# Padding SBUF arrays to one place modulo 512 bytes, and splitting MLP activations of a K tile pair together, in a two-layer decoder trunk

## The chip, the cores and the metric

One core of one Trainium2 chip runs the whole kernel. The metric is the device time in microseconds of that core, as the median of timed runs. The profile is one more execution, taken by the hardware profiler.

## What is computed

The input x is 256 tokens by 2048 features in float32. Two layers run, each with a mixer and a squared-ReLU MLP, and every sub-layer ends in x <- LN(alpha x + f(x)).

```python
bcu = x @ w_in                       # 2048 -> 6144: gate_b, gate_c, u
y = causal_conv3(gate_c * u)         # depthwise, width 3
mix = (gate_b * y) @ w_out           # layer 0
mix = mla(x, shared latent k and v)  # layer 1: 16 heads, rank 512 latents, w_o 2048 -> 2048
mlp(x) = square(relu(x @ w1)) @ w2   # 2048 -> 8192 -> 2048, both layers
```

The weights are read once: some 381 MB of float32 in 512 KB blocks.

## The kernel before

**Two-part numbers.** Every float32 operand of a large product is split into a high part, cast to float32r, and a low part, the rest (`split`, L109, and `put_split`, L306): one cast on ACT and one subtraction on DVE. A product then takes hi x hi, lo x hi and hi x lo and drops lo x lo.

**Weights.** `stream` (L64 to L83) lists all weight blocks in the order of use. `take` (L171) hands out the next ones and prepares blocks some way ahead (LOOK, 5): `load_raw` issues the DMA on SP's queue into one of five raw buffers, and `split` fills one of eight hi and eight lo buffers of 128 x 1024.

**Up products.** `products` (L230) computes one 128-feature tile after another with the weight block stationary. The activations lie as 512 columns, the high half beside the low one, so `high` (L190) streams 512 columns through the high weights and `low` (L194) 256 columns through the low weights: a pair of matmuls for each of the 16 K tiles. Their PSUM tile is ps_u.

**MLP.** `mlp` (L523) runs eight stages q of 1024 hidden features. In a stage, eight up tiles (K from xhl) are evacuated by `hidden` (L558): `whole` adds the two halves of PSUM, ACT does ReLU and square, and `put_split` writes the tile h[m] of array h (tag c, high columns beside low ones). Then the down products run with the activations stationary and 512 columns of w2 moving: `dot` (L245) is three matmuls, L247 hi x hi, L248 x high by w low, L249 x low by w high. Blocks n of 512 outputs accumulate in acc through `put`.

**Fast stages.** In 13 of the 16 stages (`FAST`) the first two output blocks use seven products instead of eight of 2 x 2 blocks (Strassen's scheme in Winograd's form): `down_fast` (L287, PSUM ps_f, 84 matmuls a stage); the other two use `down` (PSUM ps_d, 96). The sums S1 to S4 of a K tile pair are made in `hidden` from the two fh tiles into sf and split into the array `forms` (tag a2). The sums of the weights, T1 to T4, are made in `prepare` (L150 to L165) from two raw loads per pair: L154 makes T1 and T3 in a third raw buffer (raw_t) as soon as the second load is there, L157 and L160 follow, and T4 is split last into its own tile t4 in the pool `fast`. The first product of a pair (factor "4") uses T4.

**The last stage.** `to_out` (L866) loads gbt, the last norm's gain and bias spread to 128 partitions: four DMAs of 512 KB from POOL's queue (L869), into the array with tag b, which xhl used until the last up matmul.

**Where the order comes from.** All instructions are recorded through a tile framework that orders each engine's queue by its own costs; waits follow from the tiles. Each engine then works its queue in that order. `Norm.prepare` (L358) puts one float32 product, mu0p (L365), on PE before a sub-layer's sums begin.

**Places in SBUF.** Pools lie one behind the other, and each tile takes its size rounded up to 32 bytes per partition. So odd sizes (vec 736 bytes, col 16, the arrays xd 16512 or 33024) shift all that follows. The place of an array's first byte modulo 512 in the two programs is:

| array (tag) | before | after |
|---|---|---|
| raw, hi, lo: weights | 384 | 128 |
| conv input xhl0, K tiles 0 to 7 (a1) and acc | 384 | 128 |
| conv input xhl0, K tiles 8 to 15, and forms (a2) | 0 | 128 |
| z, xhl of both MLPs, oT (b) | 128 | 128 |
| h, latents (c) | 384 | 128 |
| sf | 256 | 128 |
| t4 | 256 | 128 |
| xres, S, Q, fh, evac | 384 | 128 |
| ones, identity, cos, sin, mask | 352 | 128 |

A 128-column block is 512 bytes long, so every block of an array has its array's place; only xd, with rows of 2064 bytes, runs through many.

Of the kernel before, what the change touches and what calls it, by code (L numbers as in the profile page):

```python
# [9 lines left out]
F32 = mybir.dt.float32  # L10
F32R = mybir.dt.float32r
AF = mybir.ActivationFunctionType
ALU = mybir.AluOpType
# [26 lines left out]
WO_G = 3  # L40

C_G, C_B, C_CW, C_QG, C_KG, C_END = 0, 64, 128, 176, 180, 184


@with_exitstack
def trunk(ctx: ExitStack, tc: tile.TileContext, xT, vecs, w_in, w_out, w_kv, w_q, w_uk, w_uv,
# [9 lines left out]
    pmm = ctx.enter_context(tc.tile_pool(name="pmm", bufs=4, space=PS))  # L56


    def halves(w):
# [128 lines left out]
    def high(ps, w, blk, x, first):  # L188

        nc.tensor.matmul(ps, w[blk // 8][0][:, blk % 8, :], x, start=first, stop=False)  # L190
# [4 lines left out]

    def mm_run(wps, x, k0, k1, nk, tiles_first=False):
# [32 lines left out]

    def products(n, x, group=0, cuts=()):  # L230

        ws = group_of(group)
        at = [0, *cuts, NC]
        for k0, k1 in zip(at, at[1:]):
            if ws:
                mm_run(ws, x, k0, k1, NC, tiles_first=True)
        yield from [ps for _, ps in ws]
        for i in range(group, n):
            w = take()
            ps = psum("ps_u")  # L240
            mm_run([(w, ps)], x, 0, NC, NC)
            yield ps
# [8 lines left out]
    def held(x, t):  # L251

        return [x[:, o + t * P:o + (t + 1) * P] for o in (0, T)]

# [56 lines left out]

    vec = const.tile([P, C_END], F32, name="vec")
    cos_t = const.tile([P, T], F32, name="cos_t")
# [33 lines left out]
    class Norm:  # L347
# [35 lines left out]
        def widen(self, *tags):  # L383

            n = NC // len(tags)
            self.xd = []
            v = vec[:, C_G:C_G + 128].rearrange("p (v i m) -> p m i v", v=2, i=4)[:, :, self.idx, :]
            for i, tag in enumerate(tags):
                x = act.tile([P, n, 2 * W], F32R, tag=tag, name=f"xd{self.idx}_{i}")
# [74 lines left out]
    def summed(ln, pss, add, m0=0):  # L464

        for m, ps in enumerate(pss, m0):
# [7 lines left out]
    xres = act.tile([P, NC, T], F32, tag="xres", name="xres")  # L474
    xhl = [t[:, k, :] for t in [act.tile([P, NC // 2, 2 * T], F32R, tag=a, name=f"xhl0_{a}") for a in ("a1", "a2")]
           for k in range(NC // 2)]

    first = act.tile([P, 2 * GROUP, 1024], F32, tag="b", name="first")
    for half, cuts in enumerate(FIRST):
# [12 lines left out]

    zt = act.tile([P, NC, 2 * T], F32R, tag="b", name="z")
    z = [zt[:, k, :] for k in range(NC)]
    cbuf = act.tile([P, 2, 5, T + 2], F32, tag="c", name="cbuf")
    pss = products(3 * NC, xhl, GROUP, (2, 4, 8, 12))
# [26 lines left out]
    def mlp(idx, ln, begin, blocks, fast):  # L523

        xt = act.tile([P, NC, 2 * T], F32R, tag="b", name=f"xhl{idx}")
        xhl = [xt[:, k, :] for k in range(NC)]
# [19 lines left out]
        for q in range(NQ):  # L548
            ht = act.tile([P, QC, 2 * T], F32R, tag="c", name=f"h{idx}_{q}")
            h = [ht[:, k, :] for k in range(QC)]  # L550
            forms = None
            if q in FAST[idx // 2]:
                forms = act.tile([P, QC // 2, 2, 4 * P], F32R, tag="a2", name=f"forms{idx}_{q}")
            if q == NQ - 1:
                begin(block)
            pair = []

            def hidden(m, ps, evac, *func):  # L558
                f = tmp.tile([P, T], F32, tag="fh", name="fh", bufs=3)
                evac(ps, f, *func)  # L560
                if not func:
                    nc.scalar.activation(f, f, AF.Relu)  # L562
                nc.scalar.activation(f, f, AF.Square)
                put_split(h[m], f)
                pair.append(f)
                if forms is not None and m % 2:
                    (a11, a21), (a12, a22) = ((v[:, :P], v[:, P:]) for v in pair[-2:])
                    sf = fast.tile([P, 4, P], F32, tag="sf", name="sf")
                    s1, s2, s3, s4 = (sf[:, i, :] for i in range(4))
                    nc.vector.tensor_tensor(s1, a21, a22, ALU.add)  # L570
                    nc.vector.tensor_tensor(s3, a21, a11, ALU.subtract)
                    nc.vector.tensor_tensor(s2, s1, a11, ALU.subtract)
                    nc.vector.tensor_tensor(s4, a12, s2, ALU.subtract)
                    split(forms[:, m // 2, 0, :], forms[:, m // 2, 1, :], sf.rearrange("p i c -> p (i c)"))

            if q == 0:
                for m in range(QC):
# [12 lines left out]
                    if m > 0:  # L590
                        normal()
                acc = act.tile([P, 2, D], F32, tag="a1", name=f"acc{idx}")
            else:
# [57 lines left out]
    with tc.tile_pool(name="att", bufs=1) as ap:  # L651
        lat = act.tile([P, 2 * NK, 2 * T], F32R, tag="c", name="lat")
        chl, qhl = ([lat[:, k, :] for k in range(o, o + NK)] for o in (0, NK))
# [79 lines left out]
        Banks.close(banks)  # L733
        ot = act.tile([P, H, 2 * T], F32R, tag="b", name="oT")
        oT = [ot[:, k, :] for k in range(H)]
        kq, vp = (act.tile([P, NC * W], F32, tag=a, name=f"kqv{a}") for a in ("a1", "a2"))
        k2, q2, v2 = ([r[:, o:o + 1024].rearrange("p (j t) -> p j t", j=J) for o in (b, b + 1024)]
# [128 lines left out]
    def to_out(block, put, h, forms):  # L866
        gbt = act.tile([P, NB, 2 * BW], F32, tag="b", name="gbt")
        for n in range(NB):
            nc.gpsimd.dma_start(gbt[:, n, :], gb[n].partition_broadcast(P))  # L869
        stats = small.tile([P, 2, NB, 6], F32, tag="stats", name="stats", bufs=1)  # L870

# [113 lines left out]
```

## Time and profile before

| | |
|---|---|
| timed runs: median (lowest to highest) | 2053.09 us (2053.0 to 2053.85), 3 runs |
| profiled execution: span | 2049.4 us |
| DVE, ACT busy | 1662.8 us, 1194.1 us |
| mean granted TensorE clock | 0.997 |
| HBM read over the span | 381.25 MB, 187 GB/s |

The profiled execution's span runs from its first to its last instruction; the timed runs' median is 3.7 us above it. PE and PEld are TensorE's matmuls and weight loads, DVE is VectorE, ACT ScalarE, POOL GpSimd and SP SyncE, which issues nearly all DMAs. Matmuls are pipelined, so that the duration of one overlaps the next; the distance between the starts of two is the time that one costs.

### The profile page before, as it was taken

To read this page: it belongs to the slowest core of one execution; us is meant where nothing else is said; L and a number is where in the kernel's file an instruction comes from. 1 tells how busy PE (TensorE), PEld (TensorE's weight loads), DVE (VectorE), ACT (ScalarE), POOL (GpSimd) and SP (SyncE) were. 2 spreads that over 40 slices of the span, in tenths; PEclk is the share of its full clock that TensorE was granted. 3 is DMA by queue.
4 is the path that set the end of the run, shared out by engine and by line. 5 is a ranking of instruction groups with operands and counts; after the bars stand their busy time and mean duration, and the time that the engine had idled before them with its cause. 6 is when DMAs were issued, how large, how long until landed. Compare 5 with 4: busy or idle time off the path is not lost.

```text
span 2049.4 us, 30194 instructions
## 1 busy us (share of the span) xinstructions
PE 2030.6 (99%) x11208; PEld 1760.4 (86%) x11208; DVE 1662.8 (81%) x2602; ACT 1194.1 (58%) x1860; POOL 4.5 (0%) x25
## 2 busy tenths in 40 slices
PE   9999999999999999999999999999999999999997
PEld 8888888988888888888889998898888888888885
DVE  7667677678898988989788878776879888898988
ACT  6444445676566565655656665566656656566562
POOL 0000000000000000000000000000000000000000
PEclk9999999999999999999999999999999999999998
DMA  8666666564746557465755544656475664756653
GB/s 308 202 188 187 186 185 194 159 211 136 249 142 223 193 167 250 143 226 173 234 169 164 166 124 142 197 174 196 138 236 161 196 218 156 243 153 217 212 165 137
DMA packets 108003, 385.32 MB, mean 188 GB/s; under 512 B 11984, under 2 KB 13392, under 8 KB 107856
## 3 DMA queue, kind: packets, MB, share of 16 engines
q1 hardware_dynamic: 107136, 381.04, 58.7%
q0 software_dynamic: 576, 2.10, 0.3%
q8 instruction: 88, 1.44, 0.3%
q14 instruction: 59, 0.48, 0.1%
q10 hardware_dynamic: 144, 0.26, 0.0%
HBM read 381.25 MB, written 2.10 MB: 187 GB/s over the span
## 4 chain that ended last, share of the span: by engine, by line
PE 97%; DVE 1%; DMA 1%; issue 0%; ACT 0%; SPq 0%; DVEq 0%
PE ps_u L190 34%; PE ps_u L194 17%; PE ps_d L248 7%; PE ps_d L247 7%; PE ps_d L249 7%; PE ps_f L249 4%; PE ps_f L248 4%; PE ps_f L247 4%; PE ps_w L224 1%; PE ps_w L222 1%; PE ps_w L223 1%; PE ps_g L222 1%; PE ps_g L224 1%; PE ps_g L223 1%; PE ps_wo L190 1%; PE S L788 1%
## 5 line engine op out<-in xcount | busy, mean ns | idle before, releaser
L112 DVE TENSOR_TENSOR lo<-raw,hi 128x1024 fp32r<-128x1024 f32 x712 | 861.7, 1221 | 299.0 <-ACT hi L111 294.3
L111 ACT CAST hi<-raw 128x1024 fp32r<-128x1024 f32 x712 | 742.2, 1049 | 526.6 <-PE ps_u L190 289.5
L190 PE MATMUL ps_u<-xhl,hi 128*128 128x512 f32 x1792 | 632.2, 398 | 0.0
L194 PE MATMUL ps_u<-xhl,lo 128*128 128x256 f32 x1792 | 503.0, 281 | 0.0
L190 PEld LDWEIGHTS ps_u<-xhl,hi 128*128 128x128 f32 x1792 | 336.5, 188 | 82.3
L194 PEld LDWEIGHTS ps_u<-xhl,lo 128*128 128x128 f32 x1792 | 338.5, 189 | 0.5
L190 PE MATMUL ps_u<-xhl_a,hi 128*128 128x512 f32 x720 | 253.4, 396 | 0.0
L248 PE MATMUL ps_d<-lo,h 128*128 128x512 f32 x608 | 236.9, 390 | 0.0
L249 PE MATMUL ps_d<-hi,h 128*128 128x512 f32 x608 | 236.8, 390 | 0.0
L247 PE MATMUL ps_d<-hi,h 128*128 128x512 f32 x608 | 236.6, 389 | 0.0
L194 PE MATMUL ps_u<-xhl_a,lo 128*128 128x256 f32 x720 | 202.9, 282 | 0.0
L190 PEld LDWEIGHTS ps_u<-xhl_a,hi 128*128 128x128 f32 x720 | 135.2, 188 | 31.9
L194 PEld LDWEIGHTS ps_u<-xhl_a,lo 128*128 128x128 f32 x720 | 135.8, 189 | 0.0
L248 PEld LDWEIGHTS ps_d<-lo,h 128*128 128x128 f32 x608 | 114.1, 188 | 24.2 <-DVE lo L112 0.4
L247 PEld LDWEIGHTS ps_d<-hi,h 128*128 128x128 f32 x608 | 114.2, 188 | 24.0
L249 PEld LDWEIGHTS ps_d<-hi,h 128*128 128x128 f32 x608 | 114.1, 188 | 23.9
L111 ACT CAST hi_t<-raw_t 128x1024 fp32r<-128x1024 f32 x52 | 54.8, 1054 | 77.8 <-PE ps_u L190 41.8
L190 PE MATMUL ps_u<-z,hi 128*128 128x512 f32 x256 | 89.0, 392 | 0.0
L562 ACT ACTIVATE fh<-fh 128x256 f32<-128x256 f32 x112 | 46.4, 414 | 72.0 <-DVE fh L304 72.0
L222 PE MATMUL ps_w<-xd,hi 128*128 128x258 f32 x256 | 72.5, 284 | 0.0
L224 PE MATMUL ps_w<-xd,hi 128*128 128x258 f32 x256 | 72.5, 285 | 0.0
L223 PE MATMUL ps_w<-xd,lo 128*128 128x258 f32 x256 | 72.3, 282 | 0.0
(235 smaller groups left out, 3254.8 us busy)
## 6 DMA issues: line engine op xcount, KB each, us to landing
raw<-in_w_dram SPq DMA_DIRECT2D x408, 512.0 KB, 4.4
raw<-in_w2f_dram SPq DMA_DIRECT2D x104, 512.0 KB, 3.6
raw<-in_w_in_dram SPq DMA_DIRECT2D x90, 512.0 KB, 4.2
raw<-in_w_out_dram SPq DMA_DIRECT2D x32, 512.0 KB, 3.6
raw<-in_w_o_dram SPq DMA_DIRECT2D x32, 512.0 KB, 3.9
raw<-in_w_kv_dram SPq DMA_DIRECT2D x10, 512.0 KB, 4.3
raw<-in_w_q_dram SPq DMA_DIRECT2D x8, 512.0 KB, 4.5
raw<-in_w_uk_dram SPq DMA_DIRECT2D x8, 512.0 KB, 4.4
```

Of the source, the lines that this page charges most:

```text
L111: nc.scalar.copy(hi, src)
L112: nc.vector.tensor_tensor(lo, src, hi.bitcast(F32), ALU.subtract)
L190: nc.tensor.matmul(ps, w[blk // 8][0][:, blk % 8, :], x, start=first, stop=False)
L194: nc.tensor.matmul(ps[:, :T], w[blk // 8][1][:, blk % 8, :], x[:, :T], start=False, stop=last)
L222: nc.tensor.matmul(ps[:, :W], hi, x[k][:, :W], start=k == 0, stop=False)
L223: nc.tensor.matmul(ps[:, :W], lo, x[k][:, :W], start=False, stop=False)
L224: nc.tensor.matmul(ps[:, :W], hi, x[k][:, W:], start=False, stop=k == NC - 1)
L247: nc.tensor.matmul(ps, x[0], w[0], start=first, stop=False)
L248: nc.tensor.matmul(ps, x[0], w[1], start=False, stop=False)
L249: nc.tensor.matmul(ps, x[1], w[0], start=False, stop=last)
L562: nc.scalar.activation(f, f, AF.Relu)
L788: nc.tensor.matmul(S[:, at:at + n], qp[:, tok], kp[:, :n], start=False, stop=True)
```

## The change

- `array` is new: it allocates the big arrays with a fixed room per tag, a multiple of 512 bytes, and returns a view of the wanted shape. vec, col and stats are padded as well. The scratch for software DMA shrinks from 16384 to 2048 bytes per partition.
- For stages with q >= 1, h and forms become one pair of arrays: for each K tile pair 1024 columns, two tiles of activations and the four sums, the high parts in tag c and the low parts in tag a2. The two activations and the sums lie side by side in one sf tile, and one `split` of 1024 columns (512 where the stage isn't fast) takes the place of two `put_split` of 256 and one split of 512. ReLU and square work in sf; fh with its three buffers is no longer used there, and sf has one buffer.
- gbt is loaded from SP's queue instead of POOL's.
- `mm_run` and `products` get an argument `turn`, which no call passes.

The order of the matmuls on PE is the same but for the last fast pair and a few products of the last stage: there the high halves for T4 and two more products come first, and T4's low half follows four matmuls later than before. On DVE the pair's split stands where the split of the sums stood, in the last pair ahead of L154's counterpart. On SP the four gbt loads stand between the first and the second raw load of the last fast pair.

```diff
+    ROOM = {"a1": 16896, "a2": 16896, "b": 33280, "c": 16384}
+    def array(tag, dtype, name, *dims):
+        n = int(np.prod(dims))
+        t = act.tile([P, ROOM[tag] // 4], dtype, tag=tag, name=name)[:, :n]
+        names = "uvwxyz"[:len(dims)]
+        return t.rearrange(f"p ({' '.join(names)}) -> p {' '.join(names)}", **dict(zip(names, dims)))
...
+            if k == turn:
+                low(ps, w, k, x[k], False)
+                high(ps, w, k, x[k], False)
+                continue
...
-        return [x[:, o + t * P:o + (t + 1) * P] for o in (0, T)]
+        hi, lo = x if isinstance(x, tuple) else (x[:, :T], x[:, T:])
+        return [v[:, t * P:(t + 1) * P] for v in (hi, lo)]
...
-                a[f"S{i + 1}"] = [forms[:, j, o, i * P:(i + 1) * P] for o in range(2)]
+                a[f"S{i + 1}"] = [v[:, j, (4 + i) * P:(5 + i) * P] for v in forms]
...
-    vec = const.tile([P, C_END], F32, name="vec")
+    vec = const.tile([P, 2 * P], F32, name="vec")[:, :C_END]
...
-    col = const.tile([P, 4], F32, name="col")
+    col = const.tile([P, COL], F32, name="col")
...
-            ht = act.tile([P, QC, 2 * T], F32R, tag="c", name=f"h{idx}_{q}")
-            h = [ht[:, k, :] for k in range(QC)]
-            forms = None
-            if q in FAST[idx // 2]:
-                forms = act.tile([P, QC // 2, 2, 4 * P], F32R, tag="a2", name=f"forms{idx}_{q}")
+            forms = [array(a, F32R, f"h{idx}_{q}_{a}", QC // 2, 8 * P) for a in ("c", "a2")] if q else None
...
+                h = [tuple(v[:, k // 2, (k % 2) * T:(k % 2 + 1) * T] for v in forms) for k in range(QC)]
...
-                f = tmp.tile([P, T], F32, tag="fh", name="fh", bufs=3)
+                    if m % 2 == 0:
+                        state["pair"] = fast.tile([P, 8 * P], F32, tag="sf", name="sf")
+                    f = state["pair"][:, m % 2 * T:(m % 2 + 1) * T]
...
-                put_split(h[m], f)
-                    split(forms[:, m // 2, 0, :], forms[:, m // 2, 1, :], sf.rearrange("p i c -> p (i c)"))
+                    split(hi[:, :cols], lo[:, :cols], src[:, :cols])
...
-            nc.gpsimd.dma_start(gbt[:, n, :], gb[n].partition_broadcast(P))
-        stats = small.tile([P, 2, NB, 6], F32, tag="stats", name="stats", bufs=1)
+            nc.sync.dma_start(gbt[:, n, :], gb[n].partition_broadcast(P))
+        stats = small.tile([P, 2, NB, 10], F32, tag="stats", name="stats", bufs=1)[:, :, :, :6]
...
-    nc = _bacc.Bacc("TRN2", target_bir_lowering=False, num_devices=1)
+    nc = _bacc.Bacc("TRN2", target_bir_lowering=False, num_devices=1, dynamic_dma_scratch_size=2048)
```

Elsewhere `act.tile` becomes `array` with the same tag and shape (xd, xhl0, first, z, cbuf, xhl, acc, lat, oT, kqv, gbt).

More of the change, by code (lines that the diff above doesn't have):

```diff
@@ L40 @@
 WO_G = 3
+COL = 128
 C_G, C_B, C_CW, C_QG, C_KG, C_END = 0, 64, 128, 176, 180, 184
@@ L228, in group_of, with products @@
         return [(take(), psum("ps_g")) for _ in range(n)]
-    def products(n, x, group=0, cuts=()):
+    def products(n, x, group=0, cuts=(), turn=None):
         ws = group_of(group)
@@ L474, in trunk @@
     xres = act.tile([P, NC, T], F32, tag="xres", name="xres")
-    xhl = [t[:, k, :] for t in [act.tile([P, NC // 2, 2 * T], F32R, tag=a, name=f"xhl0_{a}") for a in ("a1", "a2")]
+    xhl = [t[:, k, :] for t in [array(a, F32R, f"xhl0_{a}", NC // 2, 2 * T) for a in ("a1", "a2")]
            for k in range(NC // 2)]
-    first = act.tile([P, 2 * GROUP, 1024], F32, tag="b", name="first")
+    first = array("b", F32, "first", 2 * GROUP, 1024)
     for half, cuts in enumerate(FIRST):
@@ L491, in trunk @@
     nc.sync.dma_start(vec, vecs)
-    zt = act.tile([P, NC, 2 * T], F32R, tag="b", name="z")
+    zt = array("b", F32R, "z", NC, 2 * T)
     z = [zt[:, k, :] for k in range(NC)]
-    cbuf = act.tile([P, 2, 5, T + 2], F32, tag="c", name="cbuf")
+    cbuf = array("c", F32, "cbuf", 2, 5, T + 2)
     pss = products(3 * NC, xhl, GROUP, (2, 4, 8, 12))
@@ L523, in mlp @@
     def mlp(idx, ln, begin, blocks, fast):
-        xt = act.tile([P, NC, 2 * T], F32R, tag="b", name=f"xhl{idx}")
+        xt = array("b", F32R, f"xhl{idx}", NC, 2 * T)
         xhl = [xt[:, k, :] for k in range(NC)]
@@ L563, in hidden @@
                 nc.scalar.activation(f, f, AF.Square)
-                put_split(h[m], f)
[L565 to L573, printed above, removed]
-                    split(forms[:, m // 2, 0, :], forms[:, m // 2, 1, :], sf.rearrange("p i c -> p (i c)"))
+                if forms is None:
+                    put_split(h[m], f)
+                elif m % 2:
+                    hi, lo = (v[:, m // 2, :] for v in forms)
+                    src, cols = state["pair"], 4 * P
+                    if q in FAST[idx // 2]:
+                        cols = 8 * P
+                        a11, a21, a12, a22, s1, s2, s3, s4 = (src[:, i * P:(i + 1) * P] for i in range(8))
+                        nc.vector.tensor_tensor(s1, a21, a22, ALU.add)
+                        nc.vector.tensor_tensor(s3, a21, a11, ALU.subtract)
+                        nc.vector.tensor_tensor(s2, s1, a11, ALU.subtract)
+                        nc.vector.tensor_tensor(s4, a12, s2, ALU.subtract)
+                    split(hi[:, :cols], lo[:, :cols], src[:, :cols])
             if q == 0:
```

24 lines of the change are left out of this document (15 added, 9 removed).

## The prediction

> **What bounds the kernel now.** I read the page first: span, busy shares, and the chain that ended last.
>
> ```profile
> span 2049.4 us, 30194 instructions
> ...
> PE 2030.6 (99%) x11208; PEld 1760.4 (86%) x11208; DVE 1662.8 (81%) x2602; ACT 1194.1 (58%) x1860; POOL 4.5 (0%) x25
> ...
> PE 97%; DVE 1%; DMA 1%; issue 0%; ACT 0%; SPq 0%; DVEq 0%
> ```
>
> The chain lies on PE almost from end to end. So an instruction saved on DVE or ACT is worth nothing unless PE waits for it; what counts is how close together PE starts its matmuls, and the few places where it waits. Sums are made against the span of 2049.4; the three timed runs have their median at 2053.09, 3.7 us above, and I carry every difference over to that unchanged.
>
> Second, the timeline of one MLP stage (columns: start, duration, engine, line, tiles). Matmuls overlap, so I take distances between starts.
>
> ```profile
> 1423.55 0.39 PE L190 MATMUL ps_u<-xhl,hi 128*128 128x512 f32 x1
> ...
> 1468.76 0.39 PE L247 MATMUL ps_f<-t,h 128*128 128x512 f32 x1
> ...
> 1488.26 0.40 PE L247 MATMUL ps_d<-hi,h 128*128 128x512 f32 x1
> ...
> 1510.07 0.39 PE L190 MATMUL ps_u<-xhl,hi 128*128 128x512 f32 x1
> ```
>
> Eight up tiles are 128 pairs of a 512-wide and a 256-wide matmul in 45.21 us: 353.2 ns a pair. The 84 fast products take 19.50 us, 232.1 ns each; the 96 plain ones 21.81 us, 227.2 ns each, though both are 128x128 weights with 512 columns. No idle time stands among them. The program's own layout separates the two: in the plain products both operands begin at 384 modulo 512; in the fast products 15 of 21 have one at 384 and the other at 0 (forms) or 256 (T4).
>
> Third, groups by shape (the last two numbers before the bar's end: busy us, mean ns).
>
> ```profile
> L190 PE MATMUL ps_u<-xhl,hi 128*128 128x512 f32 x1792 | 632.2, 398 | 0.0
> L247 PE MATMUL ps_d<-hi,h 128*128 128x512 f32 x608 | 236.6, 389 | 0.0
> ...
> L247 PE MATMUL ps_f<-hi_t,forms 128*128 128x512 f32 x104 | 41.0, 394 | 0.0
> ...
> L190 PE MATMUL ps_u<-z,hi 128*128 128x512 f32 x256 | 89.0, 392 | 0.0
> ```
>
> The mean durations follow the steps: 389 for plain, 394 for one kind of fast product. But z and xhl lie in the same array with the same weights, and yet 392 stands against 398. So the place is not all. The seventh stage of the first MLP shows it too, with the same xhl:
>
> ```profile
> 977.77 0.59 PE L365 MATMUL mu0p<-xres,ones 128*128 128x256 f32 x2
> 978.02 0.59 PE L190 MATMUL ps_u<-xhl,hi 128*128 128x512 f32 x1
> 978.44 0.28 PE L194 MATMUL ps_u<-xhl,lo 128*128 128x256 f32 x1
> ...
> 1022.59 0.39 PE L247 MATMUL ps_d<-hi,h 128*128 128x512 f32 x1
> ```
>
> Less the 0.2 us that the first matmul takes longer, 128 pairs in 44.37 us: 346.6 ns. The same stream runs in a tight step (346.6) or a loose one (353.2), and keeps it. Tight here followed a break (mu0p); entered straight from plain products it was loose.
>
> **The change part by part.**
>
> *Fast products at one place.* h, forms, T4 and weights now all begin at 128, as the plain products' operands have always agreed with each other. I take the plain products' steady step for the fast products: the three rows before 1423.55 in the timeline are 226.7 apart.
>
> ```profile
> 1422.87 0.39 PE L247 MATMUL ps_d<-hi,h 128*128 128x512 f32 x1
> ```
>
> (That row to 1423.55 is three matmuls in 0.68 us.) 13 fast stages x 84 = 1092 matmuls x (232.1 - 226.7) = **-5.9 us**. Bounds: 0 if place does nothing; and, if the fast products stayed at 232.1 and pulled the plain ones with them, the slow side, 1824 x 5 ns = +9. I take -5.9, the nearest row by shape and place.
> The Trainium skill, page "TensorE: Matmul & The Clock Gate", section "Step-by-step: what each phase is for", says that PE reads the stream and the next weights through two independent ports, so that loading takes no bandwidth from the running matmul. By that rule place could not matter, this term and the next would be 0, and the sum -3.4. The step of 227.2 against 232.1 speaks against it, but one pair of groups is no proof; it is a rival below.
>
> *The short convolution's input.* Its first eight K tiles lie at 384 (like the weights), the last eight at 0; now all 16 agree.
>
> ```profile
> L190 PE MATMUL ps_u<-xhl_a,hi 128*128 128x512 f32 x365 | 128.4, 395 | 0.0
> ...
> L190 PE MATMUL ps_u<-z,hi 128*128 128x512 f32 x226 | 78.4, 391 | 0.0
> ```
>
> These are windows of 128 us (30 to 158) and 78 us (288 to 366). A cut window shows one row too many: 364 pairs in 128 us is 351.6, z's 225 in 78 are 346.7. 45 tiles x 16 = 720 pairs: loose gives +1.2, tight -3.6. This stream has no break for most of its length and 12 of the 14 xhl stages are loose, so I take **+1.2**.
>
> *xhl, z, oT.* Their array moves from 128 to 128 while the weights go from 384 to 128: the difference goes from 256 to 0. I found loose and tight at 256; the input's first half, at 0, shows the same loose kind. I take no change: 0. If the 12 loose stages fell tight: 12 x 128 x 6.6 ns = -10.1. If the two tight stages fell loose: +1.7; with z and oT (29 tiles) +4.8.
>
> *Casts and splits of a pair together.*
>
> ```profile
> L309 DVE TENSOR_TENSOR h<-fh,h 128x256 fp32r<-128x256 f32 x128 | 53.4, 419 | 2.3 <-ACT h L308 1.7
> L308 ACT CAST h<-fh 128x256 fp32r<-128x256 f32 x128 | 51.7, 406 | 3.3
> L112 DVE TENSOR_TENSOR forms<-sf,forms 128x512 fp32r<-128x512 f32 x52 | 35.5, 683 | 0.0
> L111 ACT CAST forms<-sf 128x512 fp32r<-128x512 f32 x52 | 32.0, 615 | 10.4 <-DVE sf L573 10.4
> ...
> L112 DVE TENSOR_TENSOR lo<-raw,hi 128x1024 fp32r<-128x1024 f32 x712 | 861.7, 1221 | 299.0 <-ACT hi L111 294.3
> L111 ACT CAST hi<-raw 128x1024 fp32r<-128x1024 f32 x712 | 742.2, 1049 | 526.6 <-PE ps_u L190 289.5 <-DMA raw<-in_w_dram 139.4 <-PE ps_d L249 38.2
> ```
>
> In the 14 stages with q >= 1, 112 splits of 256 and 52 of 512 become 52 of 1024 and 4 of 512. DVE: 112 x 0.419 + 52 x 0.683 = 82.4 less 52 x 1.221 + 4 x 0.683 = 66.2: 16 us saved; ACT by the same sum 77.5 less 57.0: 20 us. All of it lies beside PE: **0**. What is new is a wait: both halves of a pair and its sums share one sf buffer (it had three fh buffers), so the first add of the next pair waits in DVE's queue for the last pair's split, and weight splits stand behind it. The cover is the weights prepared ahead and DVE's spare time:
>
> ```profile
> core 0: us, PE busy (x) PEld busy (x) DVE busy (x) ACT busy (x) POOL busy (x), PEclk, DMA share, GB/s
> 1423.60:1468.70 45.10, 45.10 (x257) 39.13 (x256) 35.06 (x55) 28.64 (x50) 0.00 (x0) 1.00 0.47 137
> ...
> L248 PEld LDWEIGHTS ps_d<-lo,h 128*128 128x128 f32 x608 | 114.1, 188 | 24.2 <-DVE lo L112 0.4
> ```
>
> Ten of 45 us are free on DVE in the up part, and the plain products waited 0.4 us in all for a weight. A pair takes two tiles, 11.3 us, against 1.05 + 1.22 for its split. If the cover were gone, 2.3 us a pair; see the rivals.
>
> *gbt from POOL to SP.* Its four loads wait for the last up matmul of the last stage. Order on SP: they stand behind the first and ahead of the second raw load of the last fast pair.
>
> From the DMA view of 1985 to 2006 (GB/s in 40 slices of 0.5 us) and gbt's own:
>
> ```profile
> GB/s 0 0 0 0 0 0 0 0 86 187 335 343 47 0 257 328 211 258 390 351 390 375 343 359 390 453 382 351 414 390 414 429 304 179 47 23 0 0 0 0
> ...
> L869 POOL DMA_DIRECT2D gbt<-in_gb_dram x4: 527/529/664, 1991.0 to 1992.7; - x4
> ```
>
> The timeline of DVE and of PE behind it:
>
> ```profile
> 2001.80 1.23 DVE L154 TENSOR_TENSOR raw_t<-raw,raw 128x1024 f32<-128x1024 f32 x1 [3.39 <-DMA raw<-in_w2f_dram]
> ...
> 2005.61 0.68 DVE L112 TENSOR_TENSOR forms<-sf,forms 128x512 fp32r<-128x512 f32 x1
> ...
> 2007.34 0.68 DVE L112 TENSOR_TENSOR t<-raw,t 128x512 fp32r<-128x512 f32 x1
> ...
> 2004.97 0.40 PE L249 MATMUL ps_f<-hi_t,forms 128*128 128x512 f32 x1
> 2006.15 0.50 PE L247 MATMUL ps_f<-t,h 128*128 128x512 f32 x1 [0.78 <-ACT t L111]
> 2008.08 0.55 PE L248 MATMUL ps_f<-t,h 128*128 128x512 f32 x1 [1.44 <-DVE t L112]
> ...
> 2011.83 0.39 PE L248 MATMUL ps_f<-lo,h 128*128 128x512 f32 x1
> ```
>
> That stretch as a window (PEclk is the third number from the end), and a lone load (last number: us to landing):
>
> ```profile
> 2005.00:2012.00 7.00, 4.78 (x13) 3.30 (x12) 6.81 (x8) 4.03 (x5) 0.00 (x0) 0.76 0.65 199
> ...
> raw<-in_w2f_dram SPq DMA_DIRECT2D x104, 512.0 KB, 3.6
> ```
>
> DVE idles 3.4 us for that raw load, T4 comes late, PE waits twice, and its granted clock falls to 0.76 in the stretch. From 2004.97 to 2011.83 stand 11 starts in 6.86 us for 2.55 at 232.1: 4.3 us lost, the one large wait on PE. Today gbt's and the raw's packets mix. On one queue four gbt loads and the raw are 2.62 MB behind each other; at the 380 GB/s of the full slices a lone load of 0.52 MB is 1.4 us of transfer and 2.2 of the rest. That makes 1991.0 + 2.2 + 6.9 = 2000.1 (an estimate), 1.7 us earlier than 2001.80. The forms split, 0.68 us within the way from there to T4, goes ahead of it in DVE's new order, and PE's new order takes T4's low half four matmuls (0.9 us) later. 1.7 + 0.7 + 0.9 = 3.3 stand against waits of 0.78 + 1.44, so little of them is left, and with them goes most of the clock's fall. Bounds: 0, and -4.3. I take **-3.4**, as what is late next are the last raw loads, which PE then reaches sooner.
> The Trainium skill, page "DMA: Bandwidth & Descriptors", section "Issuing engines are not separate DMA queues", says that loads started by different engines share the same 16 engines and interleave. By it the move by itself gains nothing: a rival too.
>
> Other padding (vec, col, stats, cbuf) and the smaller DMA scratch touch nothing that PE waits for: 0; the unused `turn`: 0. xd's rows step by 2064 bytes, so its place runs through many values either way: 0.
>
> Sum: -5.9 + 1.2 - 3.4 = -8.1, so 2053.1 - 8.1 = **2045.0 us**; with the input tight 2040.2, with z, oT and both tight stages loose 2049.8.
>
> **The rivals.**
>
> 1. *Place does nothing.* The fast products are slower for another reason (their seven short groups change banks and operands more often). Only gbt counts: 2053.1 - 3.4 = 2049.7. For it: z against xhl, one place and two steps. Against: within one stage, 232.1 turns into 227.2 with the operands' places.
> 2. *gbt gains nothing.* 2.1 MB ahead of the raw load on its own queue hold it as mixed packets did: 2045.0 + 3.4 = 2048.4. For: the bytes are the same. Against: DVE's and PE's new order alone give 1.6 us.
> 3. *The loose stages fall tight.* 2045.0 - 10.1 = 2034.9. For: the step is a matter of how a stream is entered, and places move. Against: its entry, plain products at one place, stays as it is.
> 4. *Slower: the single sf buffer blocks DVE's queue.* The add of the next pair holds back the weight splits. One exposed split (1.05 + 1.22) in each of 13 stages is +29.5: 2074.5. It decides from 8.1 / 52 = 0.16 us a pair. Against: 10 free us and 11.3 us a pair, above.
>
> **How the numbers follow.** Forecast 0.60, rivals 0.12, 0.10, 0.10, 0.08. 0.2% is 4.1 us, about what a measurement of this kernel can tell from no change: faster means under 2049.0. Faster: 0.60 + 0.10 + 0.10 = 0.80; same 0.12; slower 0.08. The range leaves out rivals 3 and 4 (0.18) and takes in the forecast's own 2040.2 to 2049.8 and rivals 1 and 2: 2040.0 to 2050.0.
>
> **What would show it.** Right: ps_f's groups at about 390 ns instead of 394 to 400, the fast part of a stage at 19.0 us instead of 19.5; xhl_a at 398; xhl at 398 and z at 392; no idle of over 1 us on PE near 2000, with PEclk 1.00 there; DVE's busy time down by 16 us, ACT's by 20, and PE untouched by it. Wrong: ps_f unchanged; xhl at 392 (rival 3); DVE queued behind sf with PE waiting for lo (rival 4); T4 late again (rival 2).

## The result and the profile after

The changed kernel takes 2045.09 us (median of 4 runs, 2043.49 to 2048.57) against 2053.32 (2053.0 to 2053.85) before: ratio 0.9959, 95% interval 0.9945 to 0.9973. The forecast was 2045.0. The time is right; several terms of the sum are off by 1 to 3 us, and their errors cancel. The page of the profile after, its first lines and the groups (busy us, mean ns of one):

```profile
span 2046.4 us, 30055 instructions
...
PE 2027.4 (99%) x11208; PEld 1758.7 (86%) x11208; DVE 1655.1 (81%) x2494; ACT 1178.2 (58%) x1752; POOL 2.3 (0%) x21
...
L200 PE MATMUL ps_u<-xhl,hi 128*128 128x512 f32 x1792 | 633.0, 398 | 0.0
...
L200 PE MATMUL ps_u<-xhl_a,hi 128*128 128x512 f32 x720 | 252.4, 397 | 0.0
...
L262 PE MATMUL ps_d<-lo,h_c 128*128 128x512 f32 x480 | 186.9, 389 | 0.0
...
L200 PE MATMUL ps_u<-z,hi 128*128 128x512 f32 x256 | 90.5, 399 | 0.0
...
L262 PE MATMUL ps_f<-lo,h_c 128*128 128x512 f32 x208 | 81.0, 389 | 0.2 <-DVE lo L122 0.2
```

The fast products (ps_f) now have the plain products' 389 ns. z went the other way, from 392 to 399. The same in starts, in the timeline of the second MLP's first full stage:

```profile
1425.10 0.39 PE L200 MATMUL ps_u<-xhl,hi 128*128 128x512 f32 x1
...
1470.31 0.40 PE L261 MATMUL ps_f<-t,h_c 128*128 128x512 f32 x1
...
1489.42 0.39 PE L261 MATMUL ps_d<-hi,h_c 128*128 128x512 f32 x1
...
1511.18 0.39 PE L200 MATMUL ps_u<-xhl,hi 128*128 128x512 f32 x1
```

Up 45.21 us as before (353.2 ns a pair, loose); fast products 19.11 instead of 19.50, 227.5 ns each; plain ones 21.76, 226.7 each. 13 stages x 0.39 us make -5.1.

The other place is the last fast pair. PE's timeline there, then DVE's:

```profile
2004.38 0.39 PE L263 MATMUL ps_f<-hi_t,h_a 128*128 128x512 f32 x1
2004.87 0.50 PE L261 MATMUL ps_f<-t,h_c 128*128 128x512 f32 x1
2005.21 0.63 PE L261 MATMUL ps_f<-hi,h_c 128*128 128x512 f32 x2
2006.04 0.50 PE L262 MATMUL ps_f<-lo,h_c 128*128 128x512 f32 x1 [0.21 <-DVE lo L122]
...
2007.44 0.40 PE L263 MATMUL ps_f<-hi,h_a 128*128 128x512 f32 x1
...
1999.32 1.22 DVE L122 TENSOR_TENSOR h_a<-sf,h_c 128x1024 fp32r<-128x1024 f32 x1 [1.17 <-ACT h_c L121]
2001.04 1.23 DVE L164 TENSOR_TENSOR raw_t<-raw,raw 128x1024 f32<-128x1024 f32 x1 [0.50 <-DMA raw<-in_w2f_dram]
```

From 2004.38 to 2007.44 are nine starts in 3.06 us, 1.0 more than nine steps of 227; before it was 4.3 more. DVE's wait for the raw load is 0.50 us where it was 3.39, because the pair's split now stands ahead of it. The clock stays up here; it falls at another place, in the first 20 us, while the first loads land (PEclk is the third number from the end):

```profile
2004.00:2011.00 7.00, 6.69 (x28) 4.71 (x27) 6.79 (x8) 3.80 (x6) 0.00 (x0) 1.00 0.65 220
...
12.00:18.00 6.00, 5.53 (x21) 4.54 (x22) 5.40 (x11) 4.38 (x11) 0.00 (x0) 0.72 1.03 392
```

The first up tile starts at 26.92 us here, at 24.87 in the profile before and at 25.25 in a second profile of the changed kernel, whose clock stayed up:

```profile
12.00:18.00 6.00, 5.81 (x31) 4.84 (x32) 5.62 (x11) 4.88 (x12) 0.00 (x0) 1.00 1.05 398
```

So this execution is 1.7 to 2.0 us late when its up tiles begin. The fall goes with such a start in all 14 profiles of this study: the three that have it (this one, the kernel before with gbt on SP, and the weights moved by 128 bytes) begin at 26.6 to 26.9 us, the eleven others at 24.7 to 25.7. It is not all of it here, as the groups ahead of the window were already 0.7 to 1.0 us late. The late start is much of why this span is only 3.0 us below that of before, and the second one's 6.0.

### The profile page after: what moved, and what is told of

Its sections match the earlier page's. It is cut to its first block, busy times and chain, and to the rows that moved or that the text cites. A ratio compares the mean times of both kernels' runs of the same rounds, so it can differ in the third digit from the quotient of the medians.

```text
span 2046.4 us, 30055 instructions
## 1 busy us (share of the span) xinstructions
PE 2027.4 (99%) x11208; PEld 1758.7 (86%) x11208; DVE 1655.1 (81%) x2494; ACT 1178.2 (58%) x1752; POOL 2.3 (0%) x21
## 3 DMA queue, kind: packets, MB, share of 16 engines
q8 instruction: 88, 1.44, 0.3%
## 4 chain that ended last, share of the span: by engine, by line
PE 97%; DVE 1%; DMA 1%; issue 0%; ACT 0%; SPq 0%; DVEq 0%; ACTq 0%
PE ps_u L200 34%; PE ps_u L204 17%; PE ps_d L262 7%; PE ps_d L261 7%; PE ps_d L263 7%; PE ps_f L262 4%; PE ps_f L263 4%; PE ps_f L261 4%; PE ps_w L238 1%; PE ps_w L236 1%; PE ps_w L237 1%; PE ps_g L238 1%; PE ps_g L236 1%; PE ps_g L237 1%; PE ps_wo L200 1%; PE S L810 1%
## 5 line engine op out<-in xcount | busy, mean ns | idle before, releaser
L200 PE MATMUL ps_u<-xhl,hi 128*128 128x512 f32 x1792 | 633.0, 398 | 0.0
L200 PE MATMUL ps_u<-xhl_a,hi 128*128 128x512 f32 x720 | 252.4, 397 | 0.0
L262 PE MATMUL ps_d<-lo,h_c 128*128 128x512 f32 x480 | 186.9, 389 | 0.0
L261 PE MATMUL ps_d<-hi,h_c 128*128 128x512 f32 x480 | 186.8, 389 | 0.0
L263 PE MATMUL ps_d<-hi,h_a 128*128 128x512 f32 x480 | 186.6, 389 | 0.0
L262 PEld LDWEIGHTS ps_d<-lo,h_c 128*128 128x128 f32 x480 | 90.1, 188 | 19.1 <-DVE lo L122 0.4
L263 PEld LDWEIGHTS ps_d<-hi,h_a 128*128 128x128 f32 x480 | 90.1, 188 | 18.7
L261 PEld LDWEIGHTS ps_d<-hi,h_c 128*128 128x128 f32 x480 | 90.1, 188 | 18.6
L582 ACT ACTIVATE sf<-sf 128x256 f32<-128x256 f32 x112 | 46.5, 415 | 80.8 <-DVE sf L319 80.8
L200 PE MATMUL ps_u<-z,hi 128*128 128x512 f32 x256 | 90.5, 399 | 0.0
L262 PE MATMUL ps_f<-lo,h_c 128*128 128x512 f32 x208 | 81.0, 389 | 0.2 <-DVE lo L122 0.2
L263 PE MATMUL ps_f<-hi,h_a 128*128 128x512 f32 x208 | 81.1, 390 | 0.0
L261 PE MATMUL ps_f<-hi,h_c 128*128 128x512 f32 x208 | 81.0, 390 | 0.0
```

The source lines that it names most:

```text
L261: nc.tensor.matmul(ps, x[0], w[0], start=first, stop=False)
L262: nc.tensor.matmul(ps, x[0], w[1], start=False, stop=False)
L263: nc.tensor.matmul(ps, x[1], w[0], start=False, stop=last)
```

## The experiments

The theory to be tested: a matmul's step depends on how far apart its two operands begin, and the tight or loose step of an up stream on how it is entered. Ratios are to the kernel before, run on the same chip beside each group of experiments (its medians there: 2053.63, 2053.52 and 2053.39).

**Places alone.** The padded arrays, but h, fh, sf and forms split as before, and gbt on POOL.

```diff
-                    split(hi[:, :cols], lo[:, :cols], src[:, :cols])
+                put_split(h[m], f)
+                    split(forms[:, m // 2, 0, :], forms[:, m // 2, 1, :], sf.rearrange("p i c -> p (i c)"))
...
-            nc.sync.dma_start(gbt[:, n, :], gb[n].partition_broadcast(P))
+            nc.gpsimd.dma_start(gbt[:, n, :], gb[n].partition_broadcast(P))
```

> The changed kernel's padding alone: every large array begins at 128 modulo 512, but h and forms are split as in the kernel before (fh, two splits of 256 and one of 512) and gbt stays on POOL. Theory (place): the fast products take about 227 ns a step as in the changed kernel, the tail stall of about 4 us near 2005 stays, z, oT and the last stage sit in the loose step; about 2053.3 - 5 + 2 = 2050. Rival (the casts and sums that came together matter, because fewer writes of DVE and ACT run beside PE's reads): the fast products stay at 232 ns, 2053 or more.

2046.95 us (2044.46 to 2047.92), ratio 0.9964 [0.9951, 0.9978]. Its groups:

```profile
L200 PE MATMUL ps_u<-z,hi 128*128 128x512 f32 x256 | 90.5, 399 | 0.0
...
L261 PE MATMUL ps_f<-hi_t,forms 128*128 128x512 f32 x104 | 40.5, 389 | 0.0
```

The products with forms take 389 ns, not 394, and z is loose already: both come from the places, with no cast or split moved. The stall at the last fast pair stays, as expected: two starts there lie 1.56 and 1.93 us behind the ones before them. The time is 3 us under the 2050 expected; in the profile the input's tiles ahead of mu0p ran tight, which is worth 2.5 us and is taken up again under the changed kernel's second profile. The rival falls.

**Weights moved by 32, 64, 128 and 256 bytes.** The changed kernel with a tile ahead of the weight buffers; T4's tile moves with them, as do the scratch tiles behind it, which the large products don't read.

```diff
+    pad = ctx.enter_context(tc.tile_pool(name="pad", bufs=1)).tile([P, 32], F32, name="pad")
+    nc.vector.memset(pad, 0.0)
     whl = ctx.enter_context(tc.tile_pool(name="whl", bufs=WA))
```

> The changed kernel with 128 bytes of padding ahead of the weight buffers, so that every large product has its two operands 128 bytes apart modulo 256. Theory (the step depends on the difference of the two places): fast and plain products at about 232 ns (2916 x 5 = +14.6 us), up pairs at about 351 to 353 ns; about 2059 to 2062. Rival (it is the fast part's own pattern, or the place of one operand, that cost 5 ns): plain products stay at 227, 2045 to 2050.

> The changed kernel with 64 bytes of padding ahead of the weight buffers, so that the two operands of every large product are 64 bytes apart. If any difference of places costs (they must begin alike): fast and plain products at 232 ns as with 128, about 2058. If the cost lies at a half of 256 bytes alone or grows with the distance: 227 to 230 ns, 2045 to 2053.

> The changed kernel with 256 bytes of padding ahead of the weight buffers: 256 bytes apart. If the place counts modulo 256 (in the kernel before, xhl lay 256 from the weights and ran in the same two steps as now): plain and fast products at 227 ns, 2043 to 2049. If it counts modulo 512: 232 ns, about 2058.

> The changed kernel with 32 bytes of padding ahead of the weight buffers: the two operands of every large product 32 bytes apart. At 0 the step of a 512-wide product was 226.9 ns, at 64 bytes 228.9, at 128 bytes 232.4. If the cost grows with the distance: about 227.9, so 2045 + 2916 x 1.0 ns = 2048, and up pairs loose. If it starts only from 64 bytes: 227, 2043 to 2047.

From each profile, the same stage as above in starts; at 128 bytes:

```profile
1432.12 0.39 PE L202 MATMUL ps_u<-xhl,hi 128*128 128x512 f32 x1
...
1477.07 0.40 PE L263 MATMUL ps_f<-t,h_c 128*128 128x512 f32 x1
...
1496.59 0.40 PE L263 MATMUL ps_d<-hi,h_c 128*128 128x512 f32 x1
...
1518.89 0.39 PE L202 MATMUL ps_u<-xhl,hi 128*128 128x512 f32 x1
```

and at 32 bytes:

```profile
1429.91 0.40 PE L202 MATMUL ps_u<-xhl,hi 128*128 128x512 f32 x1
...
1474.29 0.40 PE L263 MATMUL ps_f<-t,h_c 128*128 128x512 f32 x1
...
1493.89 0.40 PE L263 MATMUL ps_d<-hi,h_c 128*128 128x512 f32 x1
...
1516.29 0.40 PE L202 MATMUL ps_u<-xhl,hi 128*128 128x512 f32 x1
```

Differences, divided by 128 pairs, 84 and 96 products (the first row is the changed kernel itself):

| bytes apart | ns a pair, up | fast | plain | median us | ratio to before |
|---|---|---|---|---|---|
| 0 | 353.2 | 227.5 | 226.7 | 2045.09 | 0.9959 [0.9945, 0.9973] |
| 32 | 346.7 | 233.3 | 233.3 | 2056.70 | 1.0016 [1.0007, 1.0025] |
| 64 | 353.3 | 228.9 | 229.0 | 2054.70 | 1.0007 [0.9998, 1.0016] |
| 128 | 351.2 | 232.4 | 232.3 | 2057.97 | 1.0025 [1.0016, 1.0034] |
| 256 | 353.2 | 227.4 | 226.7 | 2045.38 | 0.9961 [0.9949, 0.9974] |

At 128 bytes the plain products rise to the 232 that the fast products had before, in the same stage and order of instructions. That is the direct proof, and the rival (the fast part's own pattern) falls. Nor is it the place of one operand alone: here only the weights moved and the activations stayed, and in the kernel before the weights of 18 of the 21 fast products lay at the same 384 as those of the plain ones, which took 5 ns less. 256 bytes equal 0. At 32 bytes both kinds take more than at 64, so the cost doesn't grow with the distance, and both guesses for that run failed; all twelve up streams that follow plain products were tight there (44.38 us). At 128 bytes the up streams have one step of 351 ns and are neither loose nor tight. The steps are as the theory has them, but the times at 128 and 64 bytes missed their ranges by 1.0 us (below 2059) and 1.7 (above 2053): other streams changed too (the input behind mu0p took 118.2 and 118.9 us for 116.7), which the expectations had left out. Of the five distances tried, 0 and 256 are best for products of 512 columns.

**gbt.** The changed kernel with gbt on POOL again, and the kernel before with gbt on SP:

```diff
-            nc.sync.dma_start(gbt[:, n, :], gb[n].partition_broadcast(P))
+            nc.gpsimd.dma_start(gbt[:, n, :], gb[n].partition_broadcast(P))
```

> The changed kernel with its four gbt loads issued by POOL again. Theory (the move to SP takes the stall at the last fast pair away): a stall of 2 to 4 us near 2004 comes back, the granted clock falls there, about 2045.1 + 3.3 = 2048.4. Rival (the new order of DVE's and PE's queues at that pair is what removed it, and the queue is worth nothing): at most 1 us of waits there, 2045 to 2046.

> The kernel before with nothing changed but that the four gbt loads are issued by SP. Theory (the move is worth 3 us by itself): the waits of PE near 2005 to 2012 shrink from 4.3 us to about 1 and the granted clock there is 1.00, 2053.5 - 3.3 = 2050.2. Rival (the loads take the same bytes from the raw load ahead of them, so that the move alone gains nothing and only the changed kernel's order of the splits did): 2053 to 2054.

The first took 2048.03 us (2044.41 to 2052.43), ratio 0.9974 [0.9963, 0.9984], 2.9 more than the changed kernel and near the 2048.4 expected. PE and DVE in its timeline:

```profile
1998.23 0.39 PE L263 MATMUL ps_f<-hi_t,h_a 128*128 128x512 f32 x1
1999.97 0.50 PE L261 MATMUL ps_f<-t,h_c 128*128 128x512 f32 x1 [1.36 <-ACT t L121]
2002.01 0.51 PE L262 MATMUL ps_f<-t,h_c 128*128 128x512 f32 x1 [1.53 <-DVE t L122]
...
1995.19 1.23 DVE L164 TENSOR_TENSOR raw_t<-raw,raw 128x1024 f32<-128x1024 f32 x1 [3.52 <-DMA raw<-in_w2f_dram]
```

The second took 2050.91 us (2048.41 to 2054.16), ratio 0.9986 [0.9977, 0.9995], 2.5 less than before (3.3 expected). Its timeline:

```profile
2006.97 0.39 PE L249 MATMUL ps_f<-hi_t,forms 128*128 128x512 f32 x1
2007.24 0.50 PE L247 MATMUL ps_f<-t,h 128*128 128x512 f32 x1
2007.57 0.40 PE L247 MATMUL ps_f<-hi,h 128*128 128x512 f32 x1
2008.41 0.50 PE L248 MATMUL ps_f<-lo,h 128*128 128x512 f32 x1 [0.44 <-DVE lo L112]
...
2003.41 1.23 DVE L154 TENSOR_TENSOR raw_t<-raw,raw 128x1024 f32<-128x1024 f32 x1 [1.23 <-DMA raw<-in_w2f_dram]
```

With POOL, 1998.23 to 2002.01 are two starts in 3.78 us, 3.3 more than at 227; with SP, 2006.97 to 2008.41 are three in 1.44, 0.7 more than at 232. The move alone does take most of the stall away. But how it does so was not as I had worked it out. gbt's issues (the two times behind the colon's durations) with POOL in the changed kernel, with SP in the kernel before, and in the changed kernel itself:

```profile
L891 POOL DMA_DIRECT2D gbt<-in_gb_dram x4: 527/528/662, 1984.6 to 1986.3; - x4
```

```profile
L869 SPq DMA_DIRECT2D gbt<-in_gb_dram x4: 328/428/432, 1992.8 to 1994.1; - x4
```

```profile
L891 SPq DMA_DIRECT2D gbt<-in_gb_dram x4: 327/430/440, 1990.5 to 1991.8; - x4
```

From the first issue to raw_t, which starts when the raw load is there, are 10.6 us with POOL (1984.6 to 1995.19; 10.8 in the kernel before, 1991.0 to 2001.80), 10.6 with SP (1992.8 to 2003.41) and 10.5 in the changed kernel (1990.5 to 2001.04). SP also issues the first of them 0.2 us after the first fast product has started, POOL 0.5 us. Counted from that start (1990.51 and 1992.59 in the kernel before, 1984.11 and 1990.27 in the changed one), raw_t comes after 11.3 us with POOL and 10.8 with SP, and after 11.1 and 10.8. So the raw load lands 0.3 to 0.5 us earlier, not 1.7. Over all 14 profiles it is 11.1 to 11.3 us in the three with POOL and 10.2 to 11.0 in the eleven with SP.

What differs more is the order that the framework gave the engines along with the queue. With SP, DVE makes the pair's split while it waits for the load (its wait shrinks from 3.5 to 1.2 and 0.5 us), and PE takes T4's low half some products later; with POOL the pair's split stands behind raw_t and PE keeps the old order. In the kernel before, T4's low half is ready 17.5 us after the same start with POOL and 16.4 with SP: 0.5 of the difference is the landing, 0.7 the split of the sums that no longer stands in between. That the order paid more than the landing is read from these traces; an order changed without the queue was not tried.

The move has a price too. From the start of the last product on PE to the end of the span are 13.2 to 13.5 us in the three profiles with POOL (13.2 in the kernel before: 2036.16 to 2049.4) and 13.9 to 14.2 in the eleven with SP (14.1 in the changed kernel: 2032.26 to 2046.4). Why was not followed up.

**Swaps of two products.** The argument turn, which no call passes, swaps the pair of one K tile (256 columns ahead of 512). First at twelve different places k, one for each of twelve MLP stages; then at k = 2 in all stages, and in three tiles of the other streams; then only where a loose stream begins.

```diff
-                for m, ps in enumerate(products(QC, xhl)):
+                for m, ps in enumerate(products(QC, xhl, turn=TURNS.get((idx, q)))):
...
+TURNS = {(1, 1): 1, (1, 2): 2, (1, 3): 3, (1, 4): 4, (1, 5): 5, (1, 6): 6,
+         (3, 1): 7, (3, 2): 8, (3, 3): 10, (3, 4): 12, (3, 5): 13, (3, 6): 14}
```

> The changed kernel with the argument turn passed in twelve MLP stages (q 1 to 6 of both): in the first up tile of the stage, one K tile k takes its 256-wide product ahead of its 512-wide one; k is 1 to 6 in the first MLP, 7, 8, 10, 12, 13, 14 in the second. Theory (the loose step is a phase that the stream keeps until something breaks it): some stages fall into the tight step, 5547 ns a tile instead of 5653, 0.8 us a stage; 2045 less 0 to 10 us. Rival (the step is fixed by places and by the products ahead of the stage): all twelve stay at 5650 to 5661 ns a tile, 2045 within 0.5.

2041.72 us (2039.43 to 2042.84), ratio 0.9940 [0.9927, 0.9952]. Two stages in a row, k = 7 and k = 8:

```profile
1421.49 0.39 PE L202 MATMUL ps_u<-xhl,hi 128*128 128x512 f32 x1
...
1466.69 0.40 PE L263 MATMUL ps_f<-t,h_c 128*128 128x512 f32 x1
...
1507.55 0.39 PE L202 MATMUL ps_u<-xhl,hi 128*128 128x512 f32 x1
...
1551.98 0.39 PE L263 MATMUL ps_f<-t,h_c 128*128 128x512 f32 x1
```

45.20 us and 44.43. Of the twelve, k = 2, 5, 8 and 14 gave the tight step, 1, 3, 4, 6, 7, 10, 12 and 13 the loose one: every third place. The starts show the same period: in the loose stage of the changed kernel above, from the second pair on, three pairs take 350, 360 and 350 ns and then repeat. The stage with k = 8 begins like that, and from the third pair behind its swap on each takes 346 or 347. The rival falls; the step is a phase that the stream keeps.

> The changed kernel with the swap of the two products of a K tile (256-wide ahead of 512-wide) at k = 2 in the first up tile of every MLP stage with q from 1 to 7 (in the second tile of the first MLP's q = 7, which a float32 product opens), and at k = 2 in three tiles in a row early in the short convolution's input, z and oT. Theory (the loose step has a period of three K tiles, and a swap at its third place throws the stream into the tight step, as k = 2, 5, 8 and 14 did and 1, 3, 4, 6, 7, 10, 12, 13 did not; three tiles of 16 meet all three places): every MLP stage at 5547 ns a tile, and xhl_a, z and oT too behind their swaps; 12 x 0.83 + 0.8 + 1.4 + 1.4 + up to 2.4 us off: 2029 to 2033. Rival (a swap throws a tight stream out as well, or the place of the swap was chance): stages stay mixed, 2037 to 2045.

```diff
-            mm_run([(w, ps)], x, 0, NC, NC, turn=turn if i == 0 else None)
+            mm_run([(w, ps)], x, 0, NC, NC, turn=(turn or {}).get(i))
...
+                for m, ps in enumerate(products(QC, xhl, turn={int((idx, q) == (1, NQ - 1)): 2})):
```

2036.13 us (2035.01 to 2037.17), ratio 0.9917 [0.9903, 0.9930]: the MLP part came as expected, the rest did not, and the time is above 2033. The stage q = 7 of the first MLP, which mu0p opens, became loose behind its swap: up to the first down product it took the 45.29 us between these two starts (44.57 in the next run, without the swap).

```profile
970.67 0.59 PE L200 MATMUL ps_u<-xhl,hi 128*128 128x512 f32 x1
...
1015.96 0.40 PE L261 MATMUL ps_d<-hi,h_c 128*128 128x512 f32 x1
```

So a swap throws a tight stream into the loose step as well, and three in a row don't end tight. Hence one swap for each loose stream:

```diff
+                for m, ps in enumerate(products(QC, xhl, turn={} if (idx, q) == (1, NQ - 1) else {0: 2})):
...
+    summed(ln, products(NC, z, turn={3: 3}), residual)
```

> The changed kernel with one swap of the two products of a K tile: at k = 2 in the first up tile of every MLP stage that plain products or transposes lead into (13 stages; none in the first MLP's q = 7, which is tight already), and at k = 3 in the fourth tile of z, whose loose tiles of 5661 ns stand where that place is the third of its period. Theory (one swap at the third place of the period turns loose into tight; a swap in a tight stream turns it loose): all 14 stages and z behind its swap at 5547 ns a tile, 2045.1 less 12 x 0.83, 0.8 and 1.2 = 2033 to 2035, and lower than the run with swaps everywhere (2036.1). Rival (in z, entered by another order, the place is another): z stays at 5653, 2034 to 2036.

2033.47 us (2032.27 to 2035.78), ratio 0.9903 [0.9889, 0.9916]: the best version of this study. The up stream of the stage shown for the changed kernel, and two groups of the page:

```profile
1414.92 0.39 PE L200 MATMUL ps_u<-xhl,hi 128*128 128x512 f32 x1
...
1459.31 0.39 PE L261 MATMUL ps_f<-t,h_c 128*128 128x512 f32 x1
```

```profile
L200 PE MATMUL ps_u<-xhl,hi 128*128 128x512 f32 x1792 | 621.4, 391 | 0.0
...
L200 PE MATMUL ps_u<-z,hi 128*128 128x512 f32 x256 | 89.1, 392 | 0.0
```

44.39 us, 346.8 ns a pair, in place of 45.21; xhl's mean goes from 398 to 391 ns, z's from 399 to 392. The theory holds with its places and its size.

**The changed kernel once more.**

> The changed kernel as it is, for a second profile and more times. If the step of the short convolution's input is drawn anew in each execution (tight in the first 21 tiles of the two runs above that share its program up to there, loose in two others): 2042 to 2049 again, with a spread of some 5 us, and its first 21 tiles either at 5547 or at 5653 ns. If the spread comes from elsewhere: those tiles at 5653 as in its first profile.

2045.15 us (2041.81 to 2046.19), ratio 0.9957 [0.9943, 0.9970]; span 2043.4. The input's tiles ahead of mu0p (24, not 21 as I had written) were loose again, so these two profiles don't bear out the guess that they are drawn anew in each execution. Two other runs speak for it: with gbt on POOL, and in the run with one swap for each loose stream, PE's order up to mu0p is the same, and there those tiles were tight. A window of 128 us (30 to 158) counts 364 products of 512 columns in the first profile of the changed kernel and 369 in the run with POOL:

```profile
L200 PE MATMUL ps_u<-xhl_a,hi 128*128 128x512 f32 x364 | 128.7, 399 | 0.0
```

```profile
L200 PE MATMUL ps_u<-xhl_a,hi 128*128 128x512 f32 x369 | 128.0, 394 | 0.0
```

oT shows the draw between the two profiles of one and the same kernel, first and second:

```profile
L200 PE MATMUL ps_u<-oT,hi 128*128 128x512 f32 x208 | 73.5, 399 | 0.0
```

```profile
L200 PE MATMUL ps_u<-oT,hi 128*128 128x512 f32 x208 | 72.2, 391 | 0.0
```

The input (24 tiles of 16 pairs at 6.6 ns, 2.5 us), oT (1.3) and the start (2) are together about as large as the spread of the changed kernel's times, 2041.81 to 2048.57. What each timed run drew was not recorded, so that they make the spread is likely and not shown.

**Two sf buffers.**

```diff
-                        state["pair"] = fast.tile([P, 8 * P], F32, tag="sf", name="sf")
+                        state["pair"] = fast.tile([P, 8 * P], F32, tag="sf", name="sf", bufs=2)
```

> The changed kernel with two sf buffers instead of one. Theory (the wait for the one buffer lies under DVE's spare time and PE never sees it): no change, 2045 within the spread of the changed kernel (2041.8 to 2048.6). Rival (the wait costs something on PE): 1 us or more below that spread's middle, with fewer waits for lo or h on PE.

2043.81 us (2041.58 to 2046.45), ratio 0.9950 [0.9936, 0.9963]: within the changed kernel's spread, as the theory has it, but also 1.4 us below its middle, as the rival has it. The profile decides for the stages ahead of the last: their up, fast and plain parts take the same 45.21, 19.10 and 21.76 us with one buffer and with two, so the single buffer costs nothing there. In the last stage the up stream was tight with two buffers (44.5 us for 45.3) and the waits at the last fast pair 0.3 to 0.6 us shorter; whether the second buffer did that stays open.

## Why the prediction was right, point by point

| term | forecast us | measured us, in the profile of the changed kernel |
|---|---|---|
| fast products at one place | -5.9 | -5.1 (13 x 0.39) |
| gbt and the last fast pair | -3.4 | -3.3 (4.3 less 1.0), and +0.9 behind the last product (13.2 to 14.1) |
| input | +1.2 | -1.0 (253.4 to 252.4) |
| z | 0 | +1.5 (89.0 to 90.5) |
| oT | 0 | +1.3 or 0 (72.2 to 73.5, 72.2) |
| xhl | 0 | +0.8 (632.2 to 633.0; by the starts, all in the last stage) |
| plain products behind fast ones | 0 | -0.6 (12 x 0.05) |
| casts and splits | 0 | 0 |

**Fast products.** Right in cause; the size is 0.8 less, as the first dozen products of each fast part come in steps of up to 241 ns until the steady one sets in, so that the mean is 227.5 and not 226.7. The stage's 19.0 us was 19.1. The rule of the Trainium skill, page "TensorE: Matmul & The Clock Gate", section "Step-by-step: what each phase is for", of two independent ports, read as the prediction read it, would have all distances alike; the table of 0 to 256 bytes speaks against that reading, 226.7 against 233.3 ns.

**Input.** "This stream has no break for most of its length" failed: mu0p stands in it near 160 us, and with the new places the stream behind it is tight, 20 of 45 tiles. The rest was loose as forecast in both profiles of the changed kernel, and tight in three other runs. Before, nearly every tile of this input took 5627 ns (351.7 a pair), a step of its own between tight and loose.

**z, oT and xhl.** "I take no change: 0" failed by +3.6 in the first profile; z was loose in each run with the new places and no swap, oT in most. The bound of +4.8 held. That twelve stages entered from plain products stay loose held too, so rival 3 (2034.9) did not come by itself; the swaps then took 45.21 - 44.39 = 0.82 us from each, 9.8 in all, where the rival had priced 10.1.

**gbt.** The size at the last fast pair was right, and its first part wrong; what the move costs behind the last product was not thought of, and with it the term is -2.4. "1.7 us earlier" for the raw load was 0.3 to 0.5. The estimate reckoned that one queue would serve the load sooner than two mixed ones; the traces show it nearly as long after gbt's first issue from one queue as from two (10.6 for 10.8 us, 10.6 for 10.6). That agrees with the rule that the Trainium skill's page "DMA: Bandwidth & Descriptors" gives in "Issuing engines are not separate DMA queues", that loads of different engines share the same 16 and interleave; for the load itself rival 2 was nearly right. Most of the time came back, as far as the traces tell, through DVE's and PE's order, which rival 2 had as its counter-argument. "With them goes the clock's fall" held (1.00), though in the changed kernel with gbt on POOL the waits of 1.36 and 1.53 left it at 1.00 too, so that the fall was no sure part of the stall:

```profile
1998.00:2005.00 7.00, 4.11 (x17) 2.87 (x16) 7.00 (x7) 4.87 (x6) 0.00 (x0) 1.00 0.62 195
```

**Casts and splits.** Summed over all groups, DVE's busy times fall from 1795.7 to 1779.4 us and ACT's from 1280.3 to 1260.3, the -16 and -20 forecast. The page's busy time of DVE falls only by 7.7, because it counts time in which two overlap once. PE gained nothing by it: places alone gave 2046.95 where the changed kernel with gbt on POOL, which differs in the splits alone, gave 2048.03, and the intervals overlap; the up, fast and plain parts of the stages ahead of the last are the same 45.21, 19.10 and 21.76 us in both. Rival 4 (sf blocks DVE) did not come: PE's loads waited for lo as long as before.

```profile
L262 PEld LDWEIGHTS ps_d<-lo,h_c 128*128 128x128 f32 x480 | 90.1, 188 | 19.1 <-DVE lo L122 0.4
```

**Sum against median.** The terms make -5.5 with oT's draw of the first profile and -6.8 with the second's; the start takes back 2.0 and 0.4. That is -3.5 and -6.4 where the two spans lie 3.0 and 6.0 below that of before, but the medians lie 8.2 below. The forecast carried the 3.7 us between the span and the median of before over unchanged, and that step failed: a timed run's own span is only 1.8 us under its time in the kernel before (53 runs) and 2.1 in the changed one (2048.57 for 2046.4, 2045.5 for 2043.4). So the profile before, with 2049.4, was an execution of about 2051.2 (an estimate), 2.1 under its median and near the fast end of those 53 runs (2050.93 to 2056.73). From the second profile, 6.0 + 2.1 + 0.4 (its 2045.5 against the median of 2045.09) - 0.3 (2.1 less 1.8) make the 8.2. So the forecast's exactness to 0.1 us is luck: errors of 2 us cancelled. What makes the kernel before vary by 6 us stays open.

## What to carry to other kernels

When PE is the bound at 99%, look at the distance between the starts of its matmuls, not at its idle time: two groups of one shape whose steps differ by a few ns have a cause, and over thousands of matmuls it is worth several us. Let the stationary and the moving operand of a large product begin alike modulo 256 bytes, the best of the distances tried, and check it in the built layout, as one tile of odd size ahead shifts all behind it. When a transfer is moved to another queue, compare its landing and the engines' order apart: here the landing came 0.3 to 0.5 us sooner, the order seems to have paid more, and the end of the kernel became 0.9 us longer.

## What the runs showed of the hardware that I had not expected

- The step of a 512-column product against the distance of its operands' places is not monotonic: 226.7 ns at 0 and 256 bytes, 233.3 at 32, 229.0 at 64, 232.3 at 128. The activations stayed at one place in this series and the weights moved upward. The mechanism behind it was not tested.
- A stream of alternating products of 512 and 256 columns has two steady steps with the same operands, 346.7 and 353.2 ns a pair (places 0 or 256 bytes apart); the slower one repeats every three pairs. One pair issued the other way round moves it from one to the other: from loose to tight only at every third K tile, and from tight to loose at the one place tried. With one swap in each of 14 streams the kernel took 2033.47 us instead of 2045.15, without an instruction more or less.
